# Shift and scale from held weights in two halves, weight blocks loaded earlier, and rounding shared with ScalarE, in the first stage of a DeltaNet/HGRN2 block

## The chip, the core and the metric

The kernel runs on one core of one Trainium2 chip. The metric is the device time of one execution in microseconds (us), measured outside the profiler. Before the change the median of three runs is 2262.59 us (2262.49 to 2266.13). The profile is of one further execution, which took 2265.5 us; the span from its first to its last instruction is 2263.6 us. The engines are TensorE (PE for matrix products, PEld for its weight loads), VectorE (DVE), ScalarE (ACT), GpSimd (POOL) and SyncE (SP), which here only issues DMAs.

## What is computed

One layer of a diffusion backbone: 2048 latent and 256 context tokens of width 1024 are normalised and modulated, projected by one wide matrix, run through two recurrent branches, gated, merged and projected back. The change touches the first lines only:

```
mod   = silu(c) @ w_mod + b_mod                  # c: latent and context vector, w_mod: 1024 x 3072
shift, scale, gate = split(mod)                  # 1024 each, one set for latent, one for context
u     = layer_norm(h) * (1 + scale) + shift      # h: (2048 + 256) x 1024
z     = u @ w_in                                 # a_gate, b_gate, merge are 24 column blocks of 128
```

All products with u are made in a split form: u = uhi + ulo and w = wh + wl, each part rounded for a faster matrix mode, and three products uhi wh + ulo wh + uhi wl are summed.

## The kernel before

**Tiles.** Tokens come in four latent groups of 512 (gi 0 to 3) and one context group of 256 (gi 4); channels in eight blocks of 128 (k). For every group the kernel makes uhi[gi] and ulo[gi], 128 channels x 8 blocks x tokens, that stay on chip for all later projections.

**First stage (L230 to L377).** Small rows (c, c_ctx) come first (`load_rows`, L232), then sc = silu of both vectors, 128 x 8 x 2. The shift-and-scale product (L310 to L318) loads w_mod in 16 pieces of 128 x 1024 and, for each, streams two stretches of 512 columns past sc, whose two columns are held: the result stands as two rows of 2048 in four banks of PSUM (`pm`). They are copied to SBUF by ScalarE (L328) and turned into columns by sixteen small transposes (`pcol`, L330); VectorE adds b_mod and 1 and has `shsc` (L332, L333).

`stats(gi)` (L258) normalises a group's x tiles: VectorE makes the statistics (L269, L270), GpSimd the power -1/2 (L274), ScalarE and GpSimd one tile each of a pair (L279, L281). `modulate(gi)` (L287) then does for each k: four transposes into a PSUM tile of pool p0 (L294), one ScalarE pass that scales, shifts and writes u32 (L297), the rounding to uhi on VectorE (L299), and ulo = u32 - uhi on GpSimd for even k, on VectorE for odd k (L301). The first lists of statistics, of groups 0 and 1, are written ahead of the loop; in the loop, that of group gi + 2 is written behind `modulate(gi)`, not before the first ulo of odd k of group gi (`issue_after`, L341 to L346).

**Gate blocks.** Behind that stand the first two of the 24 gate blocks (`gate_block`, L218; `proj`, L206): `load_w` brings a 1024 x 128 block of w_in in two pieces through one buffer (ws), ScalarE rounds it to wh (L202), GpSimd makes wl (L203); 24 products per group follow (L211 to L213), the copies gt (L224, L226) and the store to gT. Then come the product for alpha and beta (psab, L419, L420), a small product pab (L428), and the twelve blocks of the convolution.

**Order.** A scheduler sets each engine's order when the kernel is built; each engine then runs its own list strictly in that order and waits on semaphores. DMAs here all stand in SP's list. So an instruction that waits holds up all that stands behind it on its engine.

Of the kernel before, what the change touches and what calls it, by code (L numbers as in the profile page):

```python
# [8 lines left out]
F32 = mybir.dt.float32  # L9
F32R = mybir.dt.float32r  # L10
U8 = mybir.dt.uint8
AF = mybir.ActivationFunctionType
ALU = mybir.AluOpType
# [3 lines left out]
P = 128  # L17
# [22 lines left out]
def block_kernel(ctx, tc, x, c, ctx_in, c_ctx, w_mod, b_mod, w_in, conv_w, a_log, dt_bias,  # L40
# [121 lines left out]
    def by_row(ap):  # L162
        return ap.rearrange("p (t r c) -> p t c r", r=GR, c=4)
# [7 lines left out]
    def by_col(ap):  # L171
        return ap.rearrange("p (t c r) -> p t c r", r=GR, c=4)
# [10 lines left out]
    def u_place(g, part, name, shape, dt):  # L183
        pl = uEp if g < 2 else uL if g < NG else uCp
        return pl.tile(shape, dt, tag=f"u{part}{g}", name=name)

    def stage(g, part):
        n = 4 if g < NG else 2
        t = u_place(g, part, f"stg{part}{g}", [P, n, D], F32)
        return [t[:, i, :] for i in range(n)]  # L190
# [2 lines left out]
    pj = [psj.enter_context(tc.tile_pool(name="pj", reuse_waits="tile", bufs=3 - PG, space=PSUM))]  # L193
    pg_ = [psj.enter_context(tc.tile_pool(name="pgp", reuse_waits="tile", bufs=1, space=PSUM)) if PG else pj[0]]

    def load_w(c0):
        wh = wpp.tile([P, KB, P], F32R, tag="wh", name="wh")
        wl = wpp.tile([P, KB, P], F32R, tag="wl", name="wl")
        for j in range(0, KB, 4):
            ws = wpp.tile([P, 4, P], F32, tag="ws", name="ws", bufs=1)  # L200
            sy.dma_start(out=ws, in_=w_in[0, j * P:(j + 4) * P, c0:c0 + P].rearrange("(k p) n -> p k n", p=P))
            ac.copy(out=wh[:, j:j + 4, :], in_=ws)  # L202
            po.tensor_tensor(out=wl[:, j:j + 4, :], in0=ws, in1=wh[:, j:j + 4, :].bitcast(F32), op=ALU.subtract)  # L203
        return wh, wl

    def proj(w, gi, pool=None, tag="pj"):  # L206
        wh, wl = w
# [10 lines left out]
    def gate_block(i, groups, psum=None, tag="pj", w=None):  # L218
        w = w or load_w(gcol[i])
        for g in groups:  # L220
            ps = proj(w, g, psum or pg_[0], tag)
            t = re.tile([P, GT], F32, tag="acc", name="gt", bufs=2)
            if g % 2:
                ac.copy(out=as_rows(t), in_=col_to_row(ps))  # L224
            else:
                ve.tensor_copy(out=as_rows(t), in_=col_to_row(ps))  # L226
            sy.dma_start(out=gT[i, :, g * GT:g * GT + GT], in_=t)


    with tc.tile_pool(name="w0", reuse_waits="tile", bufs=1, side="right") as w0, \  # L230
            tc.tile_pool(name="p0", reuse_waits="tile", bufs=4, space=PSUM) as p0:
        def load_rows(r0, parts):  # L232
            n = sum(k for k, _ in parts)
            rows = w0.tile([n, P], F32, tag="u32", name="rows", bufs=UB)
# [23 lines left out]
        def stats(gi, raw=None):  # L258
            n = 4 if gi < NG else 2
            xs = []  # L260
            st = w0.tile([P, n, 2, 6], F32, tag="st", name="st", bufs=2)
            mv = w0.tile([P, n, 2], F32, tag="mv", name="mv", bufs=2)
            rs = w0.tile([P, n], F32, tag="rs", name="rs", bufs=2)
            nm = w0.tile([P, n], F32, tag="nm", name="nm", bufs=2)
            for t in range(n):
                xn = raw[t] if raw else load_x(gi, t)
                xs.append(xn)
                for s in range(2):
                    ve.bn_stats(out=st[:, t, s, :], in_=xn[:, s * 512:s * 512 + 512])  # L269
                ve.bn_aggr(out=mv[:, t, :], in_=st[:, t])  # L270
                if t % 2:
                    ts_ = slice(t - 1, t + 1)
                    ve.tensor_scalar(out=rs[:, ts_], in0=mv[:, ts_, 1], scalar1=EPS, scalar2=None, op0=ALU.add)
                    po.tensor_tensor(out=rs[:, ts_], in0=rs[:, ts_], in1=nhalf.to_broadcast([P, 2]), op=ALU.pow)  # L274
                    ve.scalar_tensor_tensor(out=nm[:, ts_], in0=mv[:, ts_, 0], scalar=-1.0, in1=rs[:, ts_],
                                            op0=ALU.mult, op1=ALU.mult)
                    for u in (t - 1, t):
                        if u % 2 == XA:
                            ac.activation(out=xs[u], in_=xs[u], func=AF.Identity, scale=rs[:, u:u + 1], bias=nm[:, u:u + 1])  # L279
                        else:  # L280
                            po.tensor_scalar(out=xs[u], in0=xs[u], scalar1=rs[:, u:u + 1], scalar2=nm[:, u:u + 1],  # L281
                                             op0=ALU.mult, op1=ALU.add)
            return xs

        mod_ins = []

        def modulate(gi, xs):  # L287
            s, n = (0, GT) if gi < NG else (1, CTX)
            uhi.append(u_place(gi, "h", f"uhi{gi}", [P, KB, n], F32R))
            ulo.append(u_place(gi, "l", f"ulo{gi}", [P, KB, n], F32R))  # L290
            for k in range(KB):
                pt = p0.tile([P, n], F32, tag="m", name="pt")
                for t in range(n // P):
                    te.transpose(pt[:, t * P:t * P + P], xs[t][:, k * P:k * P + P], ident)  # L294
                u32 = w0.tile([P, n], F32, tag="u32", name="u32", bufs=UB)
                hi, lo = uhi[gi][:, k, :], ulo[gi][:, k, :]
                ac.activation(out=by_col(u32) if gi < NG else u32, in_=by_row(pt) if gi < NG else pt, func=AF.Identity,  # L297
                              scale=shsc[:, 8 + k, s:s + 1], bias=shsc[:, k, s:s + 1])
                ve.tensor_copy(out=hi, in_=u32)  # L299
                eng = po if k % 2 == 0 else ve  # L300
                li = eng.tensor_tensor(out=lo, in0=u32, in1=hi.bitcast(F32), op=ALU.subtract)  # L301
                if k % 2:
                    mod_ins.append(li.ins)
# [1 line left out]


        place, x0 = [], []
        pm = [p0.tile([2, 512], F32, tag="m", name=f"pm{j}") for j in range(4)]
        wst = sum((stage(g, part) for g in (2, 1) for part in ("h", "l")), [])
        for k in range(KB):  # L310
            for j in range(2):
                wm = wst[2 * k + j]
                sy.dma_start(out=wm, in_=w_mod[0, k * P:k * P + P, j * D:j * D + D])
                if XO <= 2 * k + j < XO + 4 * XS and (2 * k + j - XO) % XS == 0:
                    x0.append(load_x(0, len(x0)))
                for i in range(2):
                    te.matmul(out=pm[2 * j + i], lhsT=sc[:, k, :], rhs=wm[:, i * 512:i * 512 + 512],
                              start=(k == 0), stop=(k == KB - 1))  # L318
        xs = [stats(0, x0)]
        load_rows(R_BM, [(24, b_mod.rearrange("o (k p) -> (o k) p", p=P)),  # L320
                         (60, conv_w[0].rearrange("t (k p) -> (t k) p", p=P)),
                         (16, lb_param.rearrange("l d (k p) -> (l d k) p", p=P)), (1, a_norm_g), (1, b_norm_g)])
        mrs = stage(0, "h")
        pcol = p0.tile([P, 16, 2], F32, tag="m", name="pcol")
        for j in range(2):
            mr = mrs[j][0:2]
            for i in range(2):
                ac.copy(out=mr[:, i * 512:i * 512 + 512], in_=pm[2 * j + i])  # L328
            for i in range(8):
                te.transpose(pcol[:, 8 * j + i, :], mr[:, i * P:i * P + P], ident[0:2, 0:2])  # L330
        bmc = cols[:, R_BM:R_BM + 16].unsqueeze(2).to_broadcast([P, 16, 2])
        ve.tensor_tensor(out=shsc, in0=pcol, in1=bmc, op=ALU.add)  # L332
        ve.tensor_scalar(out=shsc[:, 8:16, :], in0=shsc[:, 8:16, :], scalar1=1.0, scalar2=None, op0=ALU.add)  # L333

        if NP == 2:
            xs.append(stats(1))
        for gi in range(NG + 1):
            modulate(gi, xs[gi])
            if len(xs) < NG + 1:
                if KH >= 0 and len(xs) <= KG:  # L340
                    with tc.issue_after(mod_ins[4 * gi + KH]):  # L341
                        xs.append(stats(len(xs)))
                else:
                    xs.append(stats(len(xs)))


        sy.dma_start(out=ab_bias[:, 0], in_=a_log[0].rearrange("d h -> (d h)").partition_broadcast(P))
        sy.dma_start(out=ab_bias[:, 1], in_=dt_bias[0].rearrange("d h -> (d h)").partition_broadcast(P))
        mx = w0.tile([P, 8], F32, name="mx")
        e0 = w0.tile([P, 8], F32, name="e0")  # L350
        e1 = w0.tile([P, 8], F32, name="e1")
# [8 lines left out]
        ve.tensor_tensor(out=lb_c, in0=e0, in1=mx, op=ALU.mult)  # L360
        ve.tensor_scalar(out=lb_1, in0=lb_c, scalar1=-1.0, scalar2=1.0, op0=ALU.mult, op1=ALU.add)
        ac.activation(out=lb_l, in_=lb_1, func=AF.Ln)


        ga = w0.tile([P, D], F32, tag="xn", name="ga", bufs=XB)
# [11 lines left out]
        sy.dma_start(out=gateD, in_=gr)  # L377

    for i in range(NEARLY):
        gate_block(i, range(NG))  # L380


    with tc.tile_pool(name="ra", reuse_waits="tile", bufs=2, side="right") as ra, \
# [823 lines left out]
```

## Time and profile before

| | |
|---|---|
| median of three runs | 2262.59 us |
| the profiled execution: its own time | 2265.5 us |
| its span, first to last instruction | 2263.6 us |
| mean granted TensorE clock over the span | 0.978 |
| TensorE busy | 2155.3 us, 95% |
| VectorE, ScalarE, GpSimd busy | 1386.2, 912.6, 737.0 us |
| shsc complete | 38.4 us |
| first projection product (L211) starts | 50.1 us |
| last product for alpha and beta (L420) starts | 139.6 us |

The page gives an engine's busy time over the whole span and, in tenths, over 40 slices; the trace can be asked for tables of stretches, for groups of equal instructions, for waits, and for the instructions in order of time. A row of the latter has start and duration in us, engine, line of the kernel, operation, out<-in, partitions x elements, and how many equal ones were merged; brackets give the idle time before it and what ended it. A product in plain f32 leaves two records of load and product, one in the rounded form one.

### The profile page before, as it was taken

How to read it: one execution, taken by the hardware profiler on the slowest of the kernel's cores; microseconds unless marked ns; L12 is line 12 of the kernel's file. 1: busy time of each engine (PE TensorE's matmuls, PEld its weight loads, DVE VectorE, ACT ScalarE, POOL GpSimd, SP SyncE). 2: the span in 40 equal slices, each digit the busy share in tenths (PEclk: the TensorE clock that was granted, in tenths of full speed). 3: DMA queues.
4: the chain of work that ended last, by engine and by line, in shares of the span. 5: the costliest groups of instructions: out<-in, count | busy, mean ns of one | idle time of the engine just before them, and what ended most of it. 6: DMA issues, size and time to landing. Idle time of an engine off the chain costs nothing. (4 is left out here: it accounts for less than half of the span.)

```text
span 2263.6 us, 40408 instructions
## 1 busy us (share of the span) xinstructions
PE 2155.3 (95%) x15254; PEld 1806.4 (80%) x15254; DVE 1386.2 (61%) x3198; ACT 912.6 (40%) x2312; POOL 737.0 (33%) x736
## 2 busy tenths in 40 slices
PE   7999999999999999999999899989889988999998
PEld 2778888888888888888877777778778877888887
DVE  5927676727676777784384868764333338766564
ACT  3523222224443444442435445544454445444441
POOL 3613334312221222224544444311123224433331
PEclk9999999999999999999999999999989999999999
DMA  8312222222322323224547678877888764444432
GB/s 322 105 46 66 77 66 75 83 79 74 92 79 79 110 69 96 83 84 137 174 149 212 188 232 245 237 218 209 250 258 295 250 219 162 136 141 129 132 101 79
DMA packets 298330, 330.27 MB, mean 146 GB/s; under 512 B 77535, under 2 KB 216917, under 8 KB 298135
## 3 DMA queue, kind: packets, MB, share of 16 engines
q1 hardware_dynamic: 296119, 320.35, 45.9%
q0 software_dynamic: 2016, 7.34, 0.9%
q8 instruction: 120, 1.97, 0.4%
q14 instruction: 75, 0.61, 0.1%
HBM read 216.83 MB, written 110.79 MB: 145 GB/s over the span
## 5 line engine op out<-in xcount | busy, mean ns | idle before, releaser
L211 PE MATMUL ps<-uhi,wh 128*128 128x512 f32 (+1 forms) x1824 | 707.7, 388 | 4.1 <-DVE uhi L299 2.8
L212 PE MATMUL ps<-ulo,wh 128*128 128x512 f32 (+1 forms) x1824 | 708.0, 388 | 2.3 <-DVE ulo L301 2.0
L213 PE MATMUL ps<-uhi,wl 128*128 128x512 f32 (+1 forms) x1824 | 707.1, 388 | 0.5 <-POOL wl L203 0.5
L211 PEld LDWEIGHTS ps<-uhi,wh 128*128 128x128 f32 x1824 | 346.1, 190 | 69.9 <-DVE uhi L299 3.8
L212 PEld LDWEIGHTS ps<-ulo,wh 128*128 128x128 f32 x1824 | 346.3, 190 | 66.6 <-DVE ulo L301 3.1
L213 PEld LDWEIGHTS ps<-uhi,wl 128*128 128x128 f32 x1824 | 346.4, 190 | 64.1 <-POOL wl L203 1.0
L203 POOL TENSOR_TENSOR wl<-ws,wh 128x512 fp32r<-128x512 f32 x144 | 192.6, 1338 | 530.2 <-ACT wh L202 520.9
L202 ACT CAST wh<-ws 128x512 fp32r<-128x512 f32 x144 | 89.6, 623 | 306.1 <-DMA ws<-in_w_in_dram 211.4
L399 DVE SCALAR_TENSOR_TENSOR acc<-raw,cols,acc 128x512 f32<-128x512 f32 x192 | 153.9, 854 | 0.9
L1106 PE MATMUL py<-yh,wab 128*128 128x256 f32 x512 | 146.7, 287 | 6.3 <-DVE mg L1109 6.3
L1107 PE MATMUL py<-yl,wab 128*128 128x256 f32 x512 | 145.4, 284 | 0.5 <-POOL yl L1089 0.5
L1108 PE MATMUL py<-yh,wab 128*128 128x256 f32 x512 | 145.4, 284 | 0.0
L578 POOL TENSOR_TENSOR bg<-s,fz 128x512 f32<-128x512 f32 (+1 forms) x36 | 37.3, 1036 | 259.6 <-ACT X L558 105.7
L1125 PE MATMUL pso<-uhi,mh 128*128 128x512 f32 x256 | 103.0, 404 | 7.8 <-ACT mh L1111 3.8
L1106 PEld LDWEIGHTS py<-yh,wab 128*128 128x128 f32 x512 | 98.2, 192 | 8.6 <-DVE mg L1109 7.7
L1127 PE MATMUL pso<-uhi,ml 128*128 128x512 f32 x256 | 101.8, 398 | 0.6 <-DVE ml L1112 0.6
L1126 PE MATMUL pso<-ulo,mh 128*128 128x512 f32 x256 | 101.4, 397 | 0.0
L1107 PEld LDWEIGHTS py<-yl,wab 128*128 128x128 f32 x512 | 98.6, 193 | 1.1 <-POOL yl L1089 0.7
L1108 PEld LDWEIGHTS py<-yh,wab 128*128 128x128 f32 x512 | 98.6, 193 | 0.2
L1089 POOL TENSOR_TENSOR yl<-gt,yh 128x512 fp32r<-128x512 f32 x32 | 45.1, 1413 | 147.4 <-ACT yh L1088 147.4
L402 POOL TENSOR_TENSOR acc<-acc,sg 128x512 f32<-128x512 f32 (+1 forms) x56 | 71.5, 1295 | 46.9 <-ACT sg L401 46.9
L1099 ACT ACTIVATE mg<-mg 128x512 f32<-128x512 f32 x64 | 40.4, 632 | 110.3 <-DMA mg<-gT 110.3
(373 smaller groups left out, 4024.9 us busy)
## 6 DMA issues: line engine op xcount, KB each, us to landing
ws<-in_w_in_dram SPq DMA_DIRECT2D x144, 256.0 KB, 3.2
gT<-gt SPq DMA_DIRECT2D x96, 256.0 KB, 3.5
kv<-knvD SPq DMA_DIRECT2D x36, 512.0 KB, 5.3
kq<-qkvD SPq DMA_DIRECT2D x32, 512.0 KB, 5.9
an<-atN SPq DMA_DIRECT2D x32, 512.0 KB, 6.0
mg<-gT SPq DMA_DIRECT2D x64, 256.0 KB, 3.6
qkvD<-acc SPq DMA_DIRECT2D x48, 256.0 KB, 2.3
l<-qkvD SPq DMA_DIRECT2D x16, 768.0 KB, 5.0
```

Source lines behind the costliest of these rows:

```text
L202: ac.copy(out=wh[:, j:j + 4, :], in_=ws)
L203: po.tensor_tensor(out=wl[:, j:j + 4, :], in0=ws, in1=wh[:, j:j + 4, :].bitcast(F32), op=ALU.subtract)
L211: te.matmul(out=ps, lhsT=wh[:, k, :], rhs=uhi[gi][:, k, :], start=(k == 0), stop=False)
L212: te.matmul(out=ps, lhsT=wh[:, k, :], rhs=ulo[gi][:, k, :], start=False, stop=False)
L213: te.matmul(out=ps, lhsT=wl[:, k, :], rhs=uhi[gi][:, k, :], start=False, stop=(k == KB - 1))
L399: ve.scalar_tensor_tensor(out=a_, in0=raw[:, o + k:o + k + n], scalar=wk, in1=a_, op0=ALU.mult, op1=ALU.add)
L1106: te.matmul(out=py[:, i, :], lhsT=wh[:, k, ms_], rhs=yh[i][:, k, :], start=(k == 0), stop=False)
L1107: te.matmul(out=py[:, i, :], lhsT=wh[:, k, ms_], rhs=yl[i][:, k, :], start=False, stop=False)
L1108: te.matmul(out=py[:, i, :], lhsT=wl[:, k, ms_], rhs=yh[i][:, k, :], start=False, stop=(k == H - 1))
L1125: te.matmul(out=ps, lhsT=mh[:, k, ts_], rhs=wout[0][k][:, ns], start=(k == 0), stop=False)
L1126: te.matmul(out=ps, lhsT=mh[:, k, ts_], rhs=wout[1][k][:, ns], start=False, stop=False)
L1127: te.matmul(out=ps, lhsT=ml[:, k, ts_], rhs=wout[0][k][:, ns], start=False, stop=(k == KB - 1))
```

## The change

Four things are changed, all in the first stage.

1. Shift and scale are made in two halves of the channels (`shift_scale(half)`): each w_mod piece holds 512 columns of shift and 512 of scale; eight blocks of 128 x 128 of it are held in turn and the two columns of sc are streamed, so that the result is in columns at once. The rows pm, their copies and the small transposes are gone. One product with zeros opens each sum. `modulate(0)` is cut in two: k 0 to 3 behind the first half, k 4 to 7 behind the second.
2. `load_w` is cut into `w_part`; the two gate blocks' weights are loaded inside the first stage: the first one's two pieces between the w_mod pieces of the first half, the second one's behind the second half and behind group 0.
3. For odd k, uhi is written by a second ScalarE pass from the same PSUM tile and not rounded by VectorE from u32; ulo is made by GpSimd only for k 2 and 6, by VectorE for the rest.
4. The rows of b_mod and the other parameters are loaded first; pool p0 has three tiles of the kind used for the transposes, and two for pcol; the small lower-bound computation stands behind the last ulo; the statistics of group 1 are no longer written ahead of the loop, so that in the loop those of group gi + 1 stand behind `modulate(gi)`.

```diff
-            tc.tile_pool(name="p0", reuse_waits="tile", bufs=4, space=PSUM) as p0:
+            tc.tile_pool(name="p0", reuse_waits="tile", bufs=3, space=PSUM) as p0:
...
-            for k in range(KB):
+            for k in ks:
...
-                ve.tensor_copy(out=hi, in_=u32)
-                eng = po if k % 2 == 0 else ve
+                if k % 2 == 0:
+                    ve.tensor_copy(out=hi, in_=u32)
+                else:
+                    ac.activation(out=by_col(hi) if gi < NG else hi, in_=by_row(pt) if gi < NG else pt, func=AF.Identity,
+                                  scale=shsc[:, 8 + k, s:s + 1], bias=shsc[:, k, s:s + 1])
+                eng = po if k % 4 == 2 else ve
...
+        def shift_scale(half):
+            pcol = p0.tile([P, 2, 4, 2], F32, tag="c", name="pcol", bufs=2)
+            te.matmul(out=pcol, lhsT=ident, rhs=zero16, start=True, stop=False)
+            for k in range(KB):
+                if half == 0 and k in (0, 2):
+                    w_part(w0_, gcol[0], 2 * k)
+                wm = wst[8 * half + k].rearrange("p (j n) -> p j n", j=2)
+                sy.dma_start(out=wm, in_=w_mod[0, k * P:k * P + P, 0:2 * D].rearrange("p (j n) -> p j n", j=2)
+                             [:, :, 512 * half:512 * half + 512])
+                if half == 0 and k % 2:
                     x0.append(load_x(0, len(x0)))
-                for i in range(2):
-                    te.matmul(out=pm[2 * j + i], lhsT=sc[:, k, :], rhs=wm[:, i * 512:i * 512 + 512],
-                              start=(k == 0), stop=(k == KB - 1))
+                for j in range(2):
+                    for i in range(4):
+                        te.matmul(out=pcol[:, j, i, :], lhsT=wm[:, j, i * P:i * P + P], rhs=sc[:, k, :],
+                                  start=False, stop=(k == KB - 1 and j == 1 and i == 3))
...
+            for s in range(2):
+                ve.tensor_tensor(out=own[:, :, :, s], in0=pcol[:, :, :, s], in1=bmc, op=ALU.add)
+            ve.tensor_scalar(out=own[:, 1], in0=own[:, 1], scalar1=1.0, scalar2=None, op0=ALU.add)
...
-        if NP == 2:
-            xs.append(stats(1))
+        shift_scale(0)
+        xs = [stats(0, x0)]
+        modulate(0, xs[0], range(4))
+        shift_scale(1)
+        w_part(w1_, gcol[1], 0)
         for gi in range(NG + 1):
-            modulate(gi, xs[gi])
+            modulate(gi, xs[gi], range(KB) if gi else range(4, KB))
+            if gi == 0:
+                w_part(w1_, gcol[1], 4)
...
     for i in range(NEARLY):
-        gate_block(i, range(NG))
+        gate_block(i, range(NG), w=(w0_, w1_)[i])
```

How the built order moves is seen at two places. The first is TensorE's list from the small rows to the first projection. Before, the shift-and-scale products (L317, not shown) are followed by the small transposes (L330), the transposes of group 0 (xn) and of group 1 (stgh_281), and then by the first projection product of group 0 (uhi_309):

```order
L240 MATMUL psr<-ident,rows 128x102
L330 MATMUL pcol<-ident,stgh_253 128x2 x12
L294 MATMUL pt<-ident,xn 128x128 x8
L330 MATMUL pcol<-ident,stgh_253 128x2 x4
L294 MATMUL pt<-ident,xn 128x128 x24
L294 MATMUL pt<-ident,stgh_281 128x128 x8
L211 MATMUL ps<-uhi_309,wh 128x512
```

Now, at the same place, with stgh_154 and stgl_155 holding the w_mod pieces of the first half, stgh_156 and stgl_157 those of the second, and uhi_292 being group 0's:

```order
L340 MATMUL pcol<-sc,stgh_154 128x2 x32
L340 MATMUL pcol<-sc,stgl_155 128x2 x32
L301 MATMUL pt<-ident,xn 128x128 x12
L340 MATMUL pcol<-sc,stgh_156 128x2 x8
L301 MATMUL pt<-ident,xn 128x128 x4
L340 MATMUL pcol<-sc,stgh_156 128x2 x24
L340 MATMUL pcol<-sc,stgl_157 128x2 x32
L301 MATMUL pt<-ident,xn 128x128 x12
L217 MATMUL ps<-uhi_292,wh 128x512
```

Half of group 0's transposes now stand among the shift-and-scale products, and all 128 of these stand ahead of the first projection product.

The second place is VectorE's list, where the statistics of group 2 stand. Before (group 2's x tiles are stgh_387; uhi_309 and ulo_310 are group 0's) they lie among the roundings of group 0:

```order
L301 TENSOR_TENSOR ulo_310<-u_325,uhi_309 128x512
L299 CAST uhi_309<-u_343 128x512
L273 TENSOR_SCALAR rs<-mv 128x2
L269 BN_STATS st<-stgh_387 128x6 x2
L358 TENSOR_TENSOR mx<-e_750,e_751 128x8
L269 BN_STATS st<-stgh_387 128x6 x2
L301 TENSOR_TENSOR ulo_310<-u_343,uhi_309 128x512
```

Now (group 2's x tiles are stgh_561; uhi_483 and ulo_484 are group 1's):

```order
L307 CAST uhi_483<-u_490 128x512
L312 TENSOR_TENSOR ulo_484<-u_490,uhi_483 128x512
L312 TENSOR_TENSOR ulo_484<-u_499,uhi_483 128x512
L275 BN_STATS st<-stgh_561 128x6 x8
L307 CAST uhi_483<-u_508 128x512
L232 COPY gt<-ps 128x512
```

They have moved one group later, into group 1, and stand in one piece.

More of the change, by code (lines that the diff above doesn't have):

```diff
@@ L194, in block_kernel, with w_tiles, w_part @@
     pg_ = [psj.enter_context(tc.tile_pool(name="pgp", reuse_waits="tile", bufs=1, space=PSUM)) if PG else pj[0]]
+    def w_tiles():
+        return [wpp.tile([P, KB, P], F32R, tag=t, name=t) for t in ("wh", "wl")]
+    def w_part(w, c0, j):
+        wh, wl = w
+        ws = wpp.tile([P, 4, P], F32, tag="ws", name="ws", bufs=1)
+        sy.dma_start(out=ws, in_=w_in[0, j * P:(j + 4) * P, c0:c0 + P].rearrange("(k p) n -> p k n", p=P))
+        ac.copy(out=wh[:, j:j + 4, :], in_=ws)
+        po.tensor_tensor(out=wl[:, j:j + 4, :], in0=ws, in1=wh[:, j:j + 4, :].bitcast(F32), op=ALU.subtract)
     def load_w(c0):
-        wh = wpp.tile([P, KB, P], F32R, tag="wh", name="wh")
-        wl = wpp.tile([P, KB, P], F32R, tag="wl", name="wl")
+        w = w_tiles()
         for j in range(0, KB, 4):
[L200 to L204, printed above, removed]
+            w_part(w, c0, j)
+        return w
     def proj(w, gi, pool=None, tag="pj"):
@@ L285, in block_kernel, with modulate @@
         mod_ins = []
-        def modulate(gi, xs):
+        def modulate(gi, xs, ks=range(KB)):
             s, n = (0, GT) if gi < NG else (1, CTX)
-            uhi.append(u_place(gi, "h", f"uhi{gi}", [P, KB, n], F32R))
-            ulo.append(u_place(gi, "l", f"ulo{gi}", [P, KB, n], F32R))
-            for k in range(KB):
+            if gi == len(uhi):
+                uhi.append(u_place(gi, "h", f"uhi{gi}", [P, KB, n], F32R))
+                ulo.append(u_place(gi, "l", f"ulo{gi}", [P, KB, n], F32R))
+            for k in ks:
                 pt = p0.tile([P, n], F32, tag="m", name="pt")
@@ L307, in block_kernel @@
         place, x0 = [], []
-        pm = [p0.tile([2, 512], F32, tag="m", name=f"pm{j}") for j in range(4)]
         wst = sum((stage(g, part) for g in (2, 1) for part in ("h", "l")), [])
[L310 to L314, printed above, removed]
-                    x0.append(load_x(0, len(x0)))
-                for i in range(2):
-                    te.matmul(out=pm[2 * j + i], lhsT=sc[:, k, :], rhs=wm[:, i * 512:i * 512 + 512],
-                              start=(k == 0), stop=(k == KB - 1))
-        xs = [stats(0, x0)]
+        w0_ = w_tiles()
+        w1_ = w_tiles()
+        zero16 = w0.tile([P, 16], F32, name="zero16")
+        po.memset(zero16, 0.0)
+        def shift_scale(half):
[8 more added lines that the diff above has]
+                if half == 0 and k % 2:
+                    x0.append(load_x(0, len(x0)))
+                for j in range(2):
+                    for i in range(4):
+                        te.matmul(out=pcol[:, j, i, :], lhsT=wm[:, j, i * P:i * P + P], rhs=sc[:, k, :],
+                                  start=False, stop=(k == KB - 1 and j == 1 and i == 3))
+            own = shsc.rearrange("p (j h b) s -> p h j b s", j=2, h=2)[:, half]
+            bmc = cols[:, R_BM:R_BM + 16].rearrange("p (j h b) -> p h j b", j=2, h=2)[:, half]
+            for s in range(2):
+                ve.tensor_tensor(out=own[:, :, :, s], in0=pcol[:, :, :, s], in1=bmc, op=ALU.add)
+            ve.tensor_scalar(out=own[:, 1], in0=own[:, 1], scalar1=1.0, scalar2=None, op0=ALU.add)
         load_rows(R_BM, [(24, b_mod.rearrange("o (k p) -> (o k) p", p=P)),
@@ L322, in block_kernel @@
                          (16, lb_param.rearrange("l d (k p) -> (l d k) p", p=P)), (1, a_norm_g), (1, b_norm_g)])
[L323 to L333, printed above, removed]
-        if NP == 2:
-            xs.append(stats(1))
+        shift_scale(0)
[3 more added lines that the diff above has]
+        w_part(w1_, gcol[1], 0)
         for gi in range(NG + 1):
-            modulate(gi, xs[gi])
+            modulate(gi, xs[gi], range(KB) if gi else range(4, KB))
+            if gi == 0:
+                w_part(w1_, gcol[1], 4)
             if len(xs) < NG + 1:
@@ L348, in block_kernel @@
         sy.dma_start(out=ab_bias[:, 1], in_=dt_bias[0].rearrange("d h -> (d h)").partition_broadcast(P))
+        behind = tc.issue_after(mod_ins[-1])
+        behind.__enter__()
         mx = w0.tile([P, 8], F32, name="mx")
@@ L362, in block_kernel @@
         ac.activation(out=lb_l, in_=lb_1, func=AF.Ln)
+        behind.__exit__(None, None, None)
         ga = w0.tile([P, D], F32, tag="xn", name="ga", bufs=XB)
```

## Prediction

> **What bounds the kernel now.** I read the page's slices first, then a table of the first 152 us by stretches, then the order of time inside them.
>
> ```profile
> PE   7999999999999999999999899989889988999998
> PEclk9999999999999999999999999999989999999999
> 9.00:34.00 25.00, 25.00 (x60) 5.02 (x59) 7.92 (x18) 2.39 (x3) 3.80 (x4) 1.00 1.01 395
> 36.00:62.00 26.00, 16.62 (x86) 11.69 (x86) 24.29 (x56) 16.43 (x25) 16.63 (x13) 0.80 0.58 213
> 62.00:90.00 28.00, 22.57 (x105) 17.03 (x106) 27.34 (x49) 17.29 (x24) 23.29 (x18) 0.88 0.17 41
> 90.00:139.60 49.60, 49.60 (x234) 33.73 (x233) 25.12 (x34) 14.21 (x25) 14.02 (x15) 1.00 0.40 133
> ```
>
> The first two rows give tenths in 40 slices of 56.6 us: TensorE is full from the second slice on, so what the first stage loses or wins reaches the end almost one to one. The other rows are stretches: length, busy us of PE, PEld, DVE, ACT, POOL, then the granted clock, the DMA share and GB/s. From 9 to 34 us TensorE is full of the shift-and-scale product; from 36 to 90 it is busy 39 of 54 us at a clock of 0.80 to 0.88, because VectorE (24 of 26, 27 of 28) is late with the rounded pieces; from 90 on it is full. The change lies wholly before 90 us.
>
> ```profile
> 8.24 0.13 PEld L317 LDWEIGHTS pm<-stgh,sc 128*2 128x2 f32 x1 [0.73 <-issue]
> 9.01 0.09 PEld L317 LDWEIGHTS pm<-stgh,sc 128*2 128x2 f32 x1 [0.64 <-issue]
> 9.44 0.09 PEld L317 LDWEIGHTS pm<-stgh,sc 128*2 128x2 f32 x1 [0.34 <-issue]
> 38.25 0.16 DVE L333 TENSOR_SCALAR shsc<-shsc 128x16 f32<-128x16 f32 x1
> 50.14 0.80 PE L211 MATMUL ps<-uhi,wh 128*128 128x512 f32 x1
> 56.37 0.68 DVE L301 TENSOR_TENSOR ulo<-u,uhi 128x512 fp32r<-128x512 f32 x1
> 75.97 0.68 DVE L301 TENSOR_TENSOR ulo<-u,uhi 128x512 fp32r<-128x512 f32 x1
> 89.47 1.58 DVE L301 TENSOR_TENSOR ulo<-u,uhi 128x512 fp32r<-128x512 f32 x1
> 139.74 0.39 PE L211 MATMUL ps<-uhi,wh 128*128 128x512 f32 x1
> 139.97 0.39 PE L212 MATMUL ps<-ulo,wh 128*128 128x512 f32 x1
> ```
>
> These are the milestones: start, duration, engine and line. A product in plain f32 runs as two passes, each with its own load; one pass of 512 columns takes 0.43 us (9.01 to 9.44), so 64 passes make the 27.5 us. Shift and scale are ready at 38.4; the last ulo piece of token groups 0, 1 and 2 ends at 57.1, 76.7 and 91.1; the first projection of the next stage starts at 139.7. That last number is my yardstick.
>
> **The change, part by part: the price of a pass.** Before, two columns (sc) are held and 512 are streamed; after, 128 columns of w_mod are held and two are streamed: 128 products, 256 passes, each with a full load. No row before has that shape, so I take it from both sides.
>
> ```profile
> 145.03 3.65 PEld L428 LDWEIGHTS pab<-stack,abT 32*128 32x128 f32 x32
> 1655.81 0.97 PEld L942 LDWEIGHTS psA<-S,kq 128*128 128x128 f32 x8
> 1642.03 1.78 PEld L942 LDWEIGHTS psA<-vx,kv 128*128 128x128 f32 x8
> 145.45:148.86 3.41, 3.41 (x31) 3.38 (x31) 0.04 (x1) 1.46 (x2) 1.33 (x3) 1.00 0.17 41
> 148.71 0.19 PEld L211 LDWEIGHTS ps<-uhi,wh 128*128 128x128 f32 x1
> 149.62 0.33 PEld L211 LDWEIGHTS ps<-uhi,wh 128*128 128x128 f32 x1
> 148.86:152.27 3.41, 3.41 (x9) 2.65 (x10) 0.57 (x2) 2.20 (x4) 0.13 (x2) 0.50 0.12 36
> ```
>
> L428 is nearest in kind: plain f32, 128 columns held, only 16 streamed. Its 32 loads span 3.65 us, the last one's 0.19 included: (3.65 - 0.19)/31 = 0.112 us per pass at full clock. L942 holds 128x128 as the new product does: (0.97 - 0.19)/7 = 0.111 us per pass at full clock (1655.81), and (1.78 - 0.33)/7 = 0.207 us where the clock is half (1642.03); a load of that size lasts 0.19 us at full and 0.33 at half clock, as L211 shows at 148.71 and 149.62. So a pass costs 0.112 or 0.207 to 0.223 (twice 0.112), and **which of the two is a question of the clock**. The two stretches answer it. While L428 ran, TensorE and its loader were busy 3.41 and 3.38 of 3.41 us, and yet the next stretch of the same length was granted 0.50: some thirty loads with hardly any columns streamed did not count as work. The same is seen at the start: loads come 0.77 us apart up to 9.01 and 0.43 after it; there only 2 columns are held and 512 streamed, and the clock rises. The new product streams 2 columns per pass, fewer than L428, for the whole phase, and starts with the low clock. I take the half clock and 0.21 us, the L942 row's value rounded up a little; in L942 streaming may be part of it, which L428's doubled 0.223 bounds above.
>
> The Trainium skill, "TensorE: Matmul & The Clock Gate", section "LDWEIGHTS (loading the stationary operand)", gives columns over 1.2 GHz, which is 107 ns for 128 columns and has no clock state in it. By it 256 passes would take 27.3 us in either state, and the result would be that of rival 1. The L211 rows speak against it: 0.19 us a load at full clock and 0.33 at half. Its Part 1 says that the gate decides by windows of 3.4 us of activity; the 3.41 us stretch above agrees, but whether weight loads count is not written there, only seen here.
>
> **When the halves are done.**
>
> ```profile
> 0.82 0.42 SPq L237 DMA_DIRECT2D rows<-in_c_dram  x1
> 1.30 0.29 SPq L237 DMA_DIRECT2D rows<-in_c_ctx_dram  x1
> 1.63 1.78 SPq L313 DMA_DIRECT2D stgh<-in_w_mod_dram  x4
> 5.72 8.60 PE L317 MATMUL pm<-stgh,sc 128*2 128x512 f32 x16 [2.58 <-DMA stgh<-in_w_mod_dram]
> 17.12 1.29 DVE L269 BATCH_NORM_STATS2 st<-xn 128x6 f32<-128x512 f32 x2 [13.31 <-DMA xn<-in_x_dram]
> 28.65 0.69 DVE L269 BATCH_NORM_STATS2 st<-xn 128x6 f32<-128x512 f32 x1 [2.31 <-DMA xn<-in_x_dram]
> 85.40 1.93 PEld L294 LDWEIGHTS pt<-ident,xn 128*128 128x128 f32 x9 [0.20 <-issue]
> 35.92 0.86 PEld L294 LDWEIGHTS pt<-ident,xn 128*128 128x128 f32 x8
> ```
>
> The x tiles of 17.12 and 28.65 are the 10th and the 19th block of 512 KB: 11.53/9 = 1.28 us per block. The first w_mod block used to be there at 5.7; five small loads (b_mod to b_norm_g) now go ahead on SP at some 0.4 us (0.82 to 1.63 for two), 2.0 us, and half a block of gate weights, 0.6 us: 8.3. Half 0 then takes 128 x 0.21 = 26.9 us, to 35.2; its last block is there at 8.3 + 10.5 x 1.28 = 21.7 (seven of its own, three x tiles and half a block of weights later), so TensorE and no longer DMA is the limit. Sixteen transposes of group 0 (k 0 to 3) come between, at 1.93/9 = 0.21 us each at half clock: 3.4, to 38.6. Half 1: 26.9, to 65.5; three small VectorE operations, 0.7: **shift and scale complete at 66.2 instead of 38.4**. The gate weights loaded ahead gain nothing by themselves: in TensorE's order the first projection stands behind the last pass of half 1. What is hidden under the passes is real: k 0 to 3 of group 0, the normalisation of group 1, both weight blocks.
>
> **From there to the yardstick.**
>
> ```profile
> 38.50 2.78 ACT L297 ACTIVATE u<-pt,shsc 128x512 f32<-128x512 f32 x4 [0.53 <-DVE rs L273]
> 76.58 2.46 DVE L269 BATCH_NORM_STATS2 st<-xn 128x6 f32<-128x512 f32 x4
> 66.54 0.37 DVE L299 CAST uhi<-u 128x512 fp32r<-128x512 f32 x1
> 117.11 0.68 DVE L226 COPY gt<-ps 128x512 f32<-128x512 f32 x1
> 81.92 1.43 POOL L301 TENSOR_TENSOR ulo<-u,uhi 128x512 fp32r<-128x512 f32 x1
> 82.15 1.74 DVE L301 TENSOR_TENSOR ulo<-u,uhi 128x512 fp32r<-128x512 f32 x1
> 62.49 1.29 POOL L301 TENSOR_TENSOR ulo<-u,uhi 128x512 fp32r<-128x512 f32 x1 [0.53 <-DVE uhi L299]
> 38.56 0.69 POOL L274 TENSOR_TENSOR rs<-rs,nhalf 128x2 f32<-128x2 f32 x1 [5.89 <-DVE rs L273]
> 80.39 1.56 POOL L281 TENSOR_SCALAR xn<-xn,rs,nm 128x1024 f32<-128x1024 f32 x1 [0.18 <-issue]
> ```
>
> Group 0's other four columns: 12 transposes at half clock from 65.5 (2.6), twelve projections that the order puts ahead of the transposes of k 7 (four at 0.43, eight at 0.23: 3.5), those four (0.4), then u and uhi of k 7 on ScalarE (0.7 each: 2.78 for four) and ulo (0.68): 74.2. Group 1 is VectorE's: four casts (0.37), six ulo (0.68), eight statistics of the next group (2.46/4), a gt copy (0.68) and, estimated, 0.4 of small ones make 11.6; each ulo on POOL holds VectorE up, as at 82.15, where one lasts 1.74 instead of 0.68 and ends after POOL's own: two at 1.06, 2.1. Together 13.7, to 87.9. Rounding on ScalarE trades four casts (1.5) for two more ulo on VectorE (1.4); the gain is two POOL operations fewer (2.1), and it is in the 13.7. Group 2 pays more: the statistics used to run two groups ahead, now one, so its normalisation (two pow of 0.69 with their nm, then two tiles of 1.2 to 1.5 on POOL), its transposes and first u stand bare between group 1's last ulo and the first cast, some 5 us, less the gt copy: 18, to 105.9. Behind that TensorE is full: 120 projections left at 0.228 (27.3), 48 transposes at 0.86/8 (5.2), the alpha/beta product (64 at 0.228 and 16 at half of it, 16.4), the gate row (four passes of 0.43, 1.7): 50.6 and 0.9 of latency (estimated: two result waits) give 157.4. Against 139.7 that is **+17.7 us**. What else moves (p0 with three tiles, the bound's exponentials behind the last rounding, the zero product) is in these steps or lies under full TensorE. The profiled execution took 2265.5 us (span 2263.6), 2.9 more than the median 2262.6: so 2283.2 on its own scale, 2281 (rounded up from 2280.3) against the median.
>
> Bounds of this case: passes of 0.207 or 0.223 give -0.8 or +3.3; group 2 like before (91.1 - 76.7 = 14.4) gives -3.6; VectorE never held by POOL, two groups, -4.2; one or two further half-clock stretches of 3.41 us (each costing half) +3.4. So 2271 to 2288.
>
> **Rivals.** *1, the clock or the loads do not slow down:* a pass costs 0.112. Half 0 ends with its last block, 23.5; the fourth x tile, there at 23.0, is normalised near 27; transposes 1.7; half 1 14.3: shift and scale at 44, 5 us later than before. ScalarE's order then has the second gate block's casts ahead, whose data lie behind sixteen more blocks (44 and, once the buffer is free, 48): group 0 ends near 53, 1 at 67, 2 at 85, and 85 + 51.5 = 136.5: -3.2, 2259 (2256 to 2265). Against it stand the 0.50 stretch and the 0.33 us loads; for it, that L428 holds 32 rows only, and 128 rows may count differently. *2, it is faster:* the same full clock, and the next group's normalisation stays hidden after all, by VectorE's 13.7 per group: then group 2 ends at 80.4 and the yardstick is 131.9, -7.8, 2255 (2246 to 2258). It decides by the pass: the forecast's 17.7 are gone when shift and scale come at 48.5, that is, with 256 passes and 16 transposes ahead, at (48.5 - 8.3 - 0.7)/272 = 0.145 us each; with the normalisation hidden, 4.3 us more, at 0.161. *3, the change does not load ahead in effect* is part of the forecast, as TensorE's order shows.
>
> **How the numbers follow.** Forecast 0.76, rival 1 0.14, rival 2 0.10. About 0.2% (4.5 us) is what a measurement can tell from no change. Slower is the forecast, 0.76; rival 1 lies mostly within 0.2%, 0.11, with a rest below; with rival 2 that makes faster 0.13. The range reaches from 2258, into rival 1, to 2289; the likeliest case alone has 2271 to 2288.
>
> **What would show it.** Right: a granted clock near 0.5 until about 65 us, loads of pcol 0.21 us apart, shsc complete near 66, idle TensorE between groups 1 and 2, the next stage's first projection near 157, and unchanged spacing after it. Wrong: pcol loads 0.11 apart or a clock of 1.0 in that phase (rival 1 or 2); last ulo pieces 14 us apart or less with statistics under them; or a later stage that takes the shift back, which the slices full of TensorE speak against.

## The result, and the profile after

The changed kernel takes 2281.4 us (median of six runs, 2279.65 to 2285.8), the kernel before, run beside it, 2263.2 (six runs, 2261.22 to 2269.24). The ratio is **1.0079**, with a 95% interval of 1.0067 to 1.0091: slower by some 18 us. In a second comparison (label e14 below) the ratio was 1.0072 (1.0057 to 1.0087). The profiled execution took 2283.13 us, its span is 2281.3 us; the mean clock over the span is 0.978, as before, but its first 38.5 us, which have no record of the clock, count in it as 1.00 (see below).

The slices of TensorE and its granted clock in the page of the changed kernel, then stretches of its first 157 us (columns as in the prediction):

```profile
PE   8899999999999999999999898989989988999998
PEclk8899999999999999999999999999999999999999
```
```profile
9.00:34.00 25.00, 25.00 (x119) 25.00 (x119) 6.64 (x16) 3.00 (x3) 5.04 (x5) 1.00 1.05 388
34.00:50.00 16.00, 16.00 (x92) 16.00 (x92) 8.80 (x24) 7.63 (x10) 5.33 (x6) 0.75 0.90 346
50.00:66.00 16.00, 16.00 (x76) 15.96 (x76) 1.60 (x6) 3.47 (x6) 2.18 (x2) 0.51 0.11 20
90.00:106.00 16.00, 12.00 (x51) 9.01 (x51) 12.36 (x25) 9.26 (x13) 6.79 (x6) 0.79 0.00 0
100.42:156.33 55.91, 55.48 (x264) 38.56 (x263) 29.42 (x49) 25.74 (x43) 15.89 (x17) 0.97 0.36 118
```

TensorE and its loader are now wholly busy from 9 to 66 us, where before the product took 25 us, and from 50 to 66 nothing else has much to do (VectorE 1.6 of 16, DMA at 0.11). From 100.4 us on TensorE is full again, so the shift reaches the end. The 1.00 that the clock column shows from 9 to 34 us is no measured clock: the trace's list of clock changes begins at 38.5 us, and where it has nothing the column reads 1.00. The loads themselves tell the state there. Here are the loader's rows in order of time, then a summary of the durations (minimum, median, maximum in ns) of one group of them, then the milestones:

```profile
8.23 13.73 PEld L340 LDWEIGHTS pcol<-sc,stgh 128*128 128x128 f32 x64 [3.50 <-issue]
21.84 13.77 PEld L340 LDWEIGHTS pcol<-sc,stgl 128*128 128x128 f32 x64
35.35 2.61 PEld L301 LDWEIGHTS pt<-ident,xn 128*128 128x128 f32 x12
37.94 2.13 PEld L340 LDWEIGHTS pcol<-sc,stgh 128*128 128x128 f32 x16
49.24 13.77 PEld L340 LDWEIGHTS pcol<-sc,stgl 128*128 128x128 f32 x64
```
```profile
L340 PEld LDWEIGHTS pcol<-sc,stgl x128: 333/333/333, 21.8 to 62.7; 128*128 128x128 f32 x128
```
```profile
63.41 0.17 DVE L346 TENSOR_SCALAR shsc<-shsc 128x8 f32<-128x8 f32 x1
70.60 0.69 DVE L312 TENSOR_TENSOR ulo<-u,uhi 128x512 fp32r<-128x512 f32 x1 [3.02 <-ACT uhi L309]
73.22 4.84 DVE L275 BATCH_NORM_STATS2 st<-stgh 128x6 f32<-128x512 f32 x8
82.52 0.69 DVE L312 TENSOR_TENSOR ulo<-u,uhi 128x512 fp32r<-128x512 f32 x1
88.72 0.43 DVE L307 CAST uhi<-u 128x512 fp32r<-128x512 f32 x1 [3.52 <-ACT u L304]
99.73 0.68 DVE L312 TENSOR_TENSOR ulo<-u,uhi 128x512 fp32r<-128x512 f32 x1
156.33 0.39 PE L217 MATMUL ps<-uhi,wh 128*128 128x512 f32 x1
```

A load lasts 0.333 us, as the loads of L211 did at half clock before, and 64 of them take (13.73 - 0.33)/63 = 0.213 us each, in the first half as in the last block, where the clock is granted at 0.50 on record. Shift and scale are complete at 63.6 us instead of 38.4; the last ulo pieces of groups 0, 1 and 2 end on VectorE at 71.3, 83.2 and 100.4; the statistics of group 2 stand in one piece of 4.84 us between the roundings of group 1. The yardstick, the first projection of the next stage, moved from 139.7 to 156.3: **+16.6 us of the 18 are made in the first stage**, 25.2 are lost by later shift and scale, and the stretch behind it (92.8 instead of 101.3 us) gives 8.6 of them back.

### The profile page after: what moved, and what is told of

Its sections match the earlier page's. It is cut to its first block, busy times and chain, and to the rows that moved or that the text cites. A ratio compares the mean times of both kernels' runs of the same rounds, so it can differ in the third digit from the quotient of the medians.

```text
span 2281.3 us, 40779 instructions
## 1 busy us (share of the span) xinstructions
PE 2175.2 (95%) x15434; PEld 1852.2 (81%) x15434; DVE 1373.9 (60%) x3192; ACT 923.2 (40%) x2328; POOL 719.6 (32%) x727
```

## The experiments

Times are compared with the kernel before on the same chip, whose median was 2260.59 us beside e1 to e4, 2260.15 beside e7, e8, e10 and e11, 2261.43 beside e9 and e12, 2260.29 beside e13 and e14. Where a kernel is set against the changed one, that is taken at 1.0079 times the first of these, 2278.4, an estimate, as it did not run beside them.

**Undoing the passes (e1), the statistics (e2), both (e3).** e1 streams w_mod past the two columns again, in the same halves:

```diff
-                    for i in range(4):
-                        te.matmul(out=pcol[:, j, i, :], lhsT=wm[:, j, i * P:i * P + P], rhs=sc[:, k, :],
-                                  start=False, stop=(k == KB - 1 and j == 1 and i == 3))
+                    te.matmul(out=pm[j], lhsT=sc[:, k, :], rhs=wm[:, j, :], start=(k == 0), stop=(k == KB - 1))
...
+                ac.copy(out=mr, in_=pm[j])
+                for i in range(4):
+                    te.transpose(pcol[:, j, i, :], mr[:, i * P:i * P + P], ident[0:2, 0:2])
```

e2 writes the statistics of group 1 ahead of the loop over groups again, as before the change, and e3 has both edits:

```diff
         w_part(w1_, gcol[1], 0)
+        xs.append(stats(1))
         for gi in range(NG + 1):
```

> The changed kernel with shift and scale computed as before the change (two columns held, 512 streamed, rows copied out and transposed), but still in two halves of channels, weights ahead and rounding shared. Theory (the passes at half clock are the price): a pass of 512 columns takes 0.43 us, a half 13.8 us, so half 0 ends near 24 and half 1 near 43 (its transposes wait for the fourth x tile, near 27); shsc complete at 44 to 46 instead of 63.6, granted clock 1.0 up to there, first projection of the next stage at 137 to 142 instead of 156.3; time 2260 to 2266 us, 15 to 21 below the changed kernel, ratio to before 0.999 to 1.002. Rival (the statistics one group ahead, the rounding or the order of the weights are the price, the passes only fill time that is lost anyway): the groups still end 17 us apart from the same start, yardstick above 150, time above 2274.

> The changed kernel with one line back: the statistics run two groups ahead again, those of group 2 lying under the passes of half 1. Theory: the gap between the last ulo of group 1 and that of group 2 falls from 17.2 to 12 to 14 us, since the statistics in one piece (4.84 us on VectorE) and the bare normalisation go; shsc stays at 63.6; time 4 to 8 us below the changed kernel, 2273 to 2278. Rival (VectorE has the same work in all, so it comes elsewhere): within 1.5 us of 2281.

> Both edits: streamed shift and scale in halves, statistics two groups ahead. If the two costs are independent: e1 less 4 to 8 us, 2253 to 2261, which would be faster than the kernel before (ratio 0.996 to 0.999). If the statistics of group 2 were hidden only because the passes were slow (VectorE idle from 50 to 63 us), they now stand ahead of the rounding again and e3 is within 2 us of e1, about 2262.

| | time, us | ratio to before, 95% | shsc complete | yardstick |
|---|---|---|---|---|
| before | | 1 | 38.4 | 139.74 |
| changed | | 1.0079 (1.0067 to 1.0091) | 63.6 | 156.33 |
| e1, streamed halves | 2267.82 | 1.003 (1.002 to 1.004) | 48.6 | 140.81 |
| e2, statistics two ahead | 2270.65 | 1.0039 (1.0025 to 1.0053) | 67.1 | 154.38 |
| e3, both | 2258.92 | 0.9995 (0.9984 to 1.0006) | 50.1 | 137.01 |

The first projection of the next stage in e1, e2 and e3, one row of each trace:

```profile
140.81 0.39 PE L217 MATMUL ps<-uhi,wh 128*128 128x512 f32 x1
```
```profile
154.38 0.39 PE L217 MATMUL ps<-uhi,wh 128*128 128x512 f32 x1
```
```profile
137.01 0.39 PE L217 MATMUL ps<-uhi,wh 128*128 128x512 f32 x1
```

Each edit alone takes back about half of the loss (0.5% and 0.4%), both together all of it. That e3 would be faster than the kernel before is not shown, as its interval holds 1. In e1 shift and scale are 15 us earlier, but at 48.6 and not at 44 to 46: the order puts twelve projections of group 0 between the passes of half 1. At the yardstick e1 wins 15.5 us, in the medians some 11 where 15 to 21 were expected; where the rest of it goes is not located.

e2's yardstick is only 2 us better, because its half 1 was slower in the execution that was profiled. These are the loader's rows around its transposes:

```profile
35.73 2.61 PEld L301 LDWEIGHTS pt<-ident,xn 128*128 128x128 f32 x12
38.33 3.54 PEld L340 LDWEIGHTS pcol<-sc,stgh 128*128 128x128 f32 x16
52.73 13.77 PEld L340 LDWEIGHTS pcol<-sc,stgl 128*128 128x128 f32 x64
```

The sixteen loads behind the transposes take 3.54 us, (3.54 - 0.33)/15 = 0.214 each, where the same sixteen took 2.13 in the changed kernel: there a window at full clock (one stretch of 3.41 us, as in the prediction) followed, here none. That this comes of the execution and not of e2's edit is seen below, at e14. From shift and scale on, e2 is 5.4 us shorter (87.3 instead of 92.8). The step it was to change is seen on VectorE, in the last ulo of groups 1 and 2 of e2:

```profile
87.28 0.69 DVE L312 TENSOR_TENSOR ulo<-u,uhi 128x512 fp32r<-128x512 f32 x1
100.11 0.69 DVE L312 TENSOR_TENSOR ulo<-u,uhi 128x512 fp32r<-128x512 f32 x1
```

12.8 us lie between them, instead of 17.2. These 4.4 us are the price of statistics one group ahead. e3 shows that no slow passes are needed to win them: its stretch behind shift and scale is 86.9 us.

**Is it the clock? (e4).** Six more passes that stream 512 columns behind each w_mod block of half 1; their result goes nowhere:

```diff
+                for j in range(3 * half):
+                    te.matmul(out=fil, lhsT=ident, rhs=wm[:, j % 2, :], start=True, stop=True)
```

> The changed kernel with three more products of 128x512 (six passes of 512 columns, result not used) behind each w_mod block of half 1 alone. Theory (the clock follows streamed columns and sets the price of a load): from the full-clock window after the transposes on, streaming fills 2.6 of every 4.4 us, the clock stays at 1.0 through half 1, and the loads of pcol stand 0.112 us apart instead of 0.213; half 1 lasts 8 x (16 x 0.112 + 6 x 0.43) = 35 us, and the time is 9 to 11 us above the changed kernel. Rival (a load of 128x128 for two columns costs 0.21 us of itself): pcol loads 0.21 apart with the clock at 1.0, half 1 lasts 47 us, the time is 21 us or more above.

Two of its rows (loads of pcol in the middle of half 1, products of the filler), and the stretch they lie in:

```profile
52.10 1.75 PEld L342 LDWEIGHTS pcol<-sc,stgh 128*128 128x128 f32 x15 [0.24 <-issue]
53.80 2.82 PE L345 MATMUL fil<-stgh,ident 128*128 128x512 f32 x6
```
```profile
48.00:76.00 28.00, 28.00 (x146) 19.09 (x145) 0.38 (x3) 4.04 (x6) 4.38 (x4) 1.00 0.07 14
```

The same loads now stand (1.75 - 0.19)/14 = **0.111 us** apart. Up to 48.1 us the clock was still low, so that half 1 took 39.9 us and not 35. Nothing about them was changed; all that was put between them is six passes of 512 columns, each with a load of its own. As loads alone had 0.50, it is the streamed columns that brought the clock of 1.00, and the clock sets the price of a pass. As the filler costs more than it saves, the kernel is slower, 2289.39 us in its one run, 11 above the changed kernel, as expected.

**The other parts alone, on the kernel before.** e7 takes the shared rounding alone, e8 the weights ahead alone (`w_part` inside the first stage, nothing else), e12 the small exponentials behind the last ulo alone, e9 is e7 with e8, e11 all three. In all of them the shift-and-scale product and the order of statistics are those of before. The edit of e7 is in the diff of the change above (`hi` and `eng`); those of e8 and e12:

```diff
         for k in range(KB):
+            if k in (3, 6):
+                w_part(w0_, gcol[0], 4 * (k == 6))
...
+        w_part(w1_, gcol[1], 0)
         if NP == 2:
             xs.append(stats(1))
...
+            if gi == 0:
+                w_part(w1_, gcol[1], 4)
```
```diff
+        behind = tc.issue_after(mod_ins[-1])
+        behind.__enter__()
         mx = w0.tile([P, 8], F32, name="mx")
...
         ac.activation(out=lb_l, in_=lb_1, func=AF.Ln)
+        behind.__exit__(None, None, None)
```

> The kernel before with one part of the change alone: half of the hi pieces rounded on ScalarE from PSUM and one of four differences on GpSimd instead of two. Theory (the prediction's step: VectorE sets groups 1 and 2, four casts go and two differences come, and two GpSimd operations fewer hold VectorE up for 2.1 us less per group): first projection of the next stage 3 to 5 us earlier than 139.7, time 3 to 5 us below the kernel before (ratio 0.998 to 0.999). Rival (ScalarE's second reading of PSUM keeps the transposes' buffers and delays the normalisation that ScalarE does as well): within 1 us of before, or up to 3 us above.

> The kernel before with the two gate weight blocks loaded ahead in halves, among the w_mod blocks and the first groups, and nothing else. Theory: in the kernel before, TensorE's first projection stands at 50.1 us and is followed by waits for u and ulo, not for weights, so loading them ahead gains at most 1 us and may lose the 1.2 us that a whole block takes on the queue ahead of w_mod and x: ratio 0.9993 to 1.0007. Rival (the weights' rounding on ScalarE at 49.5 and 61.4 us stands in the way of u): 2 to 3 us faster, ratio 0.9985 to 0.999.

> The kernel before with all of the change except the form and the halves of shift and scale: weights ahead, rounding shared, the bound's exponentials behind the last rounding; statistics two groups ahead as before. Shift and scale should be complete at 38 to 40 us. In the changed kernel with both costs undone, the stretch from there to the next stage's first projection is 86.9 us instead of 101.3. If that comes of rounding, weights and exponentials, this kernel has 38.5 + 88 to 92 = 127 to 131 us, and is 9 to 13 us faster than before (ratio 0.994 to 0.996). If it comes of the halves (four channels of group 0 done ahead, statistics of two groups under a longer wait), the stretch stays at 96 to 101 and the ratio is 0.998 to 1.000.

> The kernel before with weights ahead and rounding shared, the exponentials left where they were. Weights alone gave 0.9982, rounding alone 0.9987 (not certain), both with the exponentials moved 0.9997. If the two add and the moved exponentials cost: 0.996 to 0.9975 here. If both win the same microseconds (a TensorE that waits between groups 0 and 1) : 0.998 to 0.9985. If rounding takes back what the weights win: 0.999 to 1.0005.

> The kernel before with the bound's exponentials and logarithm put behind the last rounding and nothing else. Theory (they are the part that takes back the gain): their two table loads of 1.28 us on ScalarE go from 36 and 53 us to the end of the stage, where TensorE is full, so the groups should end up to 2.5 us earlier and the time be lower by up to 2 us (0.999 to 1.000); if they cost, the next stage's first projection is not later but a later instruction on VectorE or ScalarE is, and the ratio is above 1.0007.

> The kernel before with the weights ahead and nothing else, once more: if the 0.9982 is the kernel's own, the ratio comes out between 0.997 and 0.9993; if it was chance among kernels that all lie within 0.1% of before, between 0.9993 and 1.001.

| | time, us | ratio to before, 95% | yardstick |
|---|---|---|---|
| e7, rounding | 2257.66 | 0.9987 (0.9969 to 1.0006) | 134.4 |
| e8, weights ahead | 2256.3 | 0.9982 (0.9973 to 0.9991) | 133.2 |
| e13, the same again | 2256.97 | 0.9983 (0.9972 to 0.9993) | 134.8 |
| e9, weights and rounding | 2260.84 | 0.9994 (0.9981 to 1.0008) | 134.7 |
| e12, exponentials later | 2262.1 | 1.0006 (0.9993 to 1.0019) | 138.1 |
| e11, all three | 2259.49 | 0.9997 (0.9989 to 1.0006) | 133.0 |

**Weights ahead alone are faster than both kernels**, than before by 3.9 and 3.3 us. The expectation of at most 1 us failed. First two rows of the kernel before, a pass for u on ScalarE and the rounding of the first weights behind it, then e8's first projection and its stretch from 36 to 62 us:

```profile
48.70 0.78 ACT L297 ACTIVATE u<-pt,shsc 128x512 f32<-128x512 f32 x1 [2.40 <-DVE ulo L301]
49.48 0.61 ACT L202 CAST wh<-ws 128x512 fp32r<-128x512 f32 x1
```
```profile
41.69 0.47 PE L217 MATMUL ps<-uhi,wh 128*128 128x512 f32 x1
```
```profile
36.00:62.00 26.00, 19.84 (x101) 13.57 (x99) 25.96 (x62) 19.69 (x28) 17.97 (x15) 0.93 0.67 257
```

The first projection starts at 41.7 instead of 50.1, and TensorE is busy for 19.8 of the 26 us instead of 16.6, at a granted clock of 0.93 instead of 0.80. Before, the first weights were rounded at 50.1 and the first product stood right behind: the weights had kept it waiting, not u. The weights had landed at 46.4 us (issued at 37.70, 8.7 us to landing), but their rounding stands in ScalarE's list behind a pass for u that had waited 2.40 us for a ulo of VectorE. How much of the gain is the clock, how much the earlier start, and how much that the rounding no longer stands between the passes for u (the rival), is open: e13's profile has its low stretches longer (13.7 us up to 72, against 3.4 in e8) and the yardstick 1.6 us later, but the time is the same. Rounding and exponentials show nothing certain alone, and with them the gain of the weights is no longer seen in the time, though it is at the yardstick. If something takes it back behind there, it was not found. From shift and scale (39.8) to the yardstick e11 takes 93.2 us, between the two stretches that were expected; without the halves the 86.9 of e3 are not reached. The ratio is that of the second.

**The small loads (e10).** e3 with the five small loads moved behind the fifth w_mod block:

```diff
-        load_rows(R_BM, [(24, b_mod.rearrange("o (k p) -> (o k) p", p=P)),
...
             for k in range(KB):
+                if half == 0 and k == 5:
+                    load_rows(R_BM, [(24, b_mod.rearrange("o (k p) -> (o k) p", p=P)),
...
```

> The kernel of streamed halves with statistics two ahead, and the five small loads (b_mod to the norms' gains) put behind the fifth w_mod block instead of ahead of the first. Theory: the first w_mod block is there at 5.7 instead of 8.2 us, and as the stretch up to the end of half 1 is a chain of transfers and passes, shift and scale come 1.5 to 2.5 us earlier: 2256.5 to 2258 on the same scale, ratio to before 0.998 to 0.999. Rival (half 1 waits for x and its normalisation, not for the first block): no difference from 0.9995.

The time is 2262.94 us, the ratio 1.0015 (1.0 to 1.003): not better than e3. The issue queue of SP, with start and duration, and TensorE's row that waits:

```profile
7.45 1.18 SPq L243 DMA_DIRECT2D rows<-in_b_mod_dram  x1
8.68 0.36 SPq L243 DMA_DIRECT2D rows<-in_conv_w_dram  x1
9.96 0.32 SPq L243 DMA_DIRECT2D rows<-in_lb_param_dram  x1
11.31 0.22 SPq L243 DMA_DIRECT2D rows<-in_a_norm_g_dram  x1
12.66 0.22 SPq L243 DMA_DIRECT2D rows<-in_b_norm_g_dram  x1
13.97 0.39 SPq L335 DMA_DIRECT2D stgl<-in_w_mod_dram  x1
```
```profile
23.18 5.29 PE L340 MATMUL pm<-stgl,sc 128*2 128x512 f32 x8 [3.68 <-DMA stgl<-in_w_mod_dram]
```

The first block does come earlier (first product at 6.3), but behind large transfers each small load is issued some 1.3 us after the one before it, the time of one 512 KB block. The kernel before shows the same: there the five stand behind w_mod and x and are issued from 20.96 to 26.08 us, 1.28 apart. In e10 the five hold the queue from 7.45 to 13.97, and TensorE waits 3.68 us for the next w_mod block. Half 0 ends 2.7 us later than in e3, not earlier.

**The changed kernel again (e14).**

> The changed kernel once more, beside the kernel before on the same chip. Theory (windows of 3.41 us lie differently in each execution): time again 1.007 to 1.009 of before; loads of pcol 0.333 us long and 0.213 apart in all of half 0; and in half 1, either again one window at full clock (shsc near 63.6) or none (near 67), since whether the 16 transposes fill a window depends on where it begins. If the full window belongs to the program, shsc comes at 63.4 to 63.8 again.

Ratio 1.0072 (1.0057 to 1.0087), yardstick at 156.44, and again a window at full clock in half 1 (shsc 63.65). Whether that window belongs to the program is decided by e4: up to its first filler product, at 43 us, TensorE runs the changed kernel's instructions in the same order, and yet the sixteen loads behind the transposes are these:

```profile
37.92 3.54 PEld L342 LDWEIGHTS pcol<-sc,stgh 128*128 128x128 f32 x16
```

They stand 0.21 us apart, as in e2, so there was no full window: it belongs to the execution, and the changed kernel can be without it. The span of e14, though, is 2271.0, 10 us less than that of the first profile. The stretch from 1440 to 1700 us in the first and in the second profile of the changed kernel:

```profile
1440.00:1700.00 260.00, 234.50 (x2375) 197.74 (x2374) 141.93 (x427) 123.28 (x400) 57.21 (x81) 0.95 0.76 227
```
```profile
1440.00:1700.00 260.00, 237.15 (x2419) 200.35 (x2416) 144.21 (x431) 126.54 (x412) 55.89 (x80) 0.97 0.79 235
```

Up to 1400 us equal instructions start within a microsecond of each other; in these 260 us the second does 44 products more, at a clock of 0.97 instead of 0.95. So a single profile serves for the first stage, to the 2 or 3 us that such a window moves there, and not for the total: the yardstick says where, the medians how much.

## Why the prediction was right

- **The pass price held.** 0.21 us was taken, 0.213 was measured, and e4 shows that the cause was the one given: loads don't hold the clock (0.50), streamed columns do (1.00). Rivals 1 and 2 (0.112 us per pass) needed a clock that isn't there. That 128 rows might count differently from the 32 of L428, the point in rival 1's favour, does not hold. The Trainium skill, "TensorE: Matmul & The Clock Gate", section "LDWEIGHTS (loading the stationary operand)", gives columns over 1.2 GHz and no clock state, by estimate 107 ns for 128 columns; that is near e4's 0.111 at full clock, and half of the 0.213 here.
- **Half 0 and the first block** came at 35.35 and 8.23, predicted 35.2 and 8.3.
- **Half 1 was 2.5 us too long in the sum** (65.5, measured 62.96). The sum had 0.21 us for every pass; in the profiled execution one window at full clock followed the transposes. The two windows behind them, of which the second has hardly any streaming and half the clock:

```profile
38.49:41.91 3.42, 3.42 (x33) 3.42 (x32) 3.05 (x6) 2.38 (x4) 0.00 (x0) 1.00 1.01 404
41.91:45.32 3.41, 3.41 (x18) 3.41 (x18) 3.41 (x9) 0.23 (x1) 1.27 (x1) 0.50 1.06 388
```

  Shift and scale came at 63.6 instead of 66.2. In e2, without that window, they came at 67.1, so the sum lies between two kinds of executions.
- **The groups:** 7.7, 11.9 and 17.2 us, where the sum had 8.0, 13.7 and 18. In group 1 the term for VectorE held up by GpSimd (2.1) was too large: one ulo of 1.26 instead of 0.68 is all that shows of it. The bare normalisation that the sum put at 4.3 us shows in e2 as 4.4 (17.2 less 12.8); in time e2 wins 8 (2278.4 to 2270.65), more than the bound of 3.6 us that the sum had for it, and how the rest divides was not tried.
- **Behind group 2 the sum was 4.4 us short** (51.5, measured 55.9). TensorE is full, as predicted, but 132 projections were left instead of 120, 2.7 us, and until 103.4 the clock was half, 1.5 us; of the 0.9 us of latency in the sum, 0.43 are seen as idle time. The groups of products in that stretch:

```profile
L217 PE MATMUL ps<-uhi,wh 128*128 128x512 f32 x44 | 18.0, 417 | 0.0
L218 PE MATMUL ps<-ulo,wh 128*128 128x512 f32 x44 | 17.9, 412 | 0.0
L219 PE MATMUL ps<-uhi,wl 128*128 128x512 f32 x44 | 17.9, 410 | 0.0
```

- **The closeness of the total is partly luck.** The sum had shift and scale 2.6 us too late, the three groups 2.9 too long and the rest 4.4 too short, which adds up to 1.1: 17.7 was forecast at the yardstick and 16.6 measured. That the median, 2281.4, meets the 2281 of the sum is more luck still: the ratio of e14 gives some 16 us and not 18.
- **Almost one to one to the end**, as the prediction reads from the full slices, holds only to several us. e1 is 1.1 us behind the kernel before at the yardstick and 7.2 in the median; e8 is 6.5 ahead and 3.9, e11 6.7 and 0.7. Each yardstick is one execution's.
- **Weights ahead gain nothing** fits the changed kernel, whose first projection (65.4) stands behind the last pass, though it was not tried there. On the kernel before they gain 3 to 4 us: the prediction puts TensorE's idle time from 36 us on down to VectorE alone, but until 50.1 the first product waited for weights. **Rounding** shared with ScalarE was put at 2.1 us per group; e7 is 2.5 us faster in all, and its interval holds 1.

## What to carry to other kernels

Before a product is turned round so that the wide operand is held, count what streams: with two columns per load TensorE looked full here, but the clock fell to half and a pass took 0.213 us instead of 0.111. Hold the narrow operand (e1), or give such a phase streamed work that has to be done anyway; the latter was not tried, and e4's useless work cost more than it saved. Try the parts of a change one by one: here one of them, alone on the kernel before, was worth 3 to 4 us, and it was buried under two others that cost 8 and more each. Undoing those two (e3) did not bring it to light; only the trial alone did.

## What was not expected of the hardware

A window in which the loader is busy from end to end, but hardly a column is streamed, is granted half clock next, with loads of 128 rows as with loads of 32. Twelve transposes, 2.6 us of half-clock streaming, were enough for a full window of 3.41 us in both profiles of the changed kernel (2.13 us for the next sixteen loads in the first) and not in e2 and e4 (3.54). What differs is how the windows lie. In the changed kernel one ends at 38.5 us, behind the last transpose (37.96). Counted back in steps of 3.41 us from where the recorded clock begins, at 48.1 in e4 and 72.0 in e2, one ends near 37.9 there, before the last transpose does (37.94 and 38.34). By this estimate, which rests on these executions alone, nearly all of the 2.6 us had to lie in one window. Small transfers cost an issue queue most where it is deep in large ones: five took 6.5 us of it there, and some 1.8 at the start.
